# A two-layer diffusion step on one core: up-projection halves of 320 instead of 322 columns, and two instructions queued elsewhere

## The chip, the cores and the metric

The kernel runs on one core of a Trainium2 chip. The metric is the device time of one execution in microseconds; the median of three runs before the change is 1535.12 us (1534.82 to 1535.30).

## The reference

One inference step of a two-layer trunk in float32: 512 latent tokens and 128 prompt (context) tokens of width 1024. Layer 0 mixes tokens by neighbourhood attention (NA) with a learned position bias, layer 1 by grouped-query attention (GQA) with rotary positions. After each mixer stands a gated feed-forward block (FFN) with a width-3 convolution along the tokens. Six modulation rows per layer come from a conditioning vector.

```python
def conv_ffn(h, w_up, conv_w, conv_b, w_down):       # w_up 1024 x 5632, w_down 2816 x 1024
    u = h @ w_up
    up = jnp.pad(u, ((0, 0), (1, 1), (0, 0)))
    u = up[:, :-2] * conv_w[0] + up[:, 1:-1] * conv_w[1] + up[:, 2:] * conv_w[2] + conv_b
    a, gt = jnp.split(u, 2, axis=-1)
    return (jax.nn.silu(a) * gt) @ w_down

for l in range(2):
    shift/scale/gate rows = split(silu(c) @ ada_w[l] + ada_b[l], 6)      # for c and for c_ctx
    h = rmsnorm(x, norm_mix_pre) * (1 + scale) + shift
    o = neighbourhood_attention(...) if l == 0 else gqa(...)
    x = x + gate * rmsnorm(o @ w_o, norm_mix_post)
    h = rmsnorm(x, norm_ffn_pre) * (1 + scale) + shift
    x = x + gate * rmsnorm(conv_ffn(h, ...), norm_ffn_post)
# outputs: both token groups, and the prompt's keys and values of both layers
```

The convolution pads each of the two token groups on its own: there is a zero on both sides of the latents and of the prompt.

## The kernel before

Every float32 product is made of three passes in a reduced format: each operand is split into a high part (a cast on ScalarE: `wh`, `ahi`, `oh`) and a low part (a subtraction on VectorE or GpSimd: `wl`, `alo`, `ol`), and high x high, high x low and low x high add up in one accumulator.

**Order.** The instructions of TensorE run in the order of the text (`pe` chains them). On the other engines a planner, which simulates the program, orders the ready instructions by their place in the text. `behind(a, b)` puts a behind b in its engine's queue without a wait for b's end, and `keep_in_program_order` (`pin=True` in `wsplit`) puts an instruction behind the one that stands before it in the text on its engine. All large weights come by SP's DMA queue into four rotating buffers `wr`.

**NA and its output projection.** While the heads are worked off, a stream of items (`stream`, `na_qk_items`, `na_v_items`) makes queries, keys and values of the next heads in small parts; `fill` takes one part. The last item is the keys of the last head pair. `OW` says behind which of its parts (0 to 7) the output projection's weights 0, 1 and 2 of the first column half are fetched and split (`m0.weights`): behind parts 0, 2 and 4. The last part (i = 7) copies the prompt's keys out of the accumulator (`kp`, ScalarE), for a transpose on TensorE (`tk`, in `tail`) that follows, and then forms the key tiles `kh` and `kl`.

**The up-projection.** It is a Winograd form of Strassen's scheme: the 1024 rows of the contraction and the 640 tokens are cut in halves, and value and gate columns form the third pair, so that 7 block products stand for 8. The tokens are laid out with a zero column behind the latents and behind the prompt, `GAP` = 642, and the halves have `TH` = 322 columns (2 x 322 = 644). `Halves` builds the token blocks B; the first `PLAIN` = 2 rows of chunks of 128 output columns are made without the scheme (`plain0`, `plain1`), the other 20 by the seven products (1, 2, 6, 3, 7, 5, 4 in `evict`), whose order in the loop is 6, 5, 1 of the next row, 7, 2 of the next row, 3, 4. Each product is 12 matmuls of TH columns. The results are added into `C`, [128, 4 x 322 + 3], a new tile of three rotating ones for each row, with a GpSimd memset of its three zero columns. The columns of the gap come out as zeros since the token columns there are zero.

**Around the products.** For each row p, VectorE forms sums of weight blocks in place (`block_sums`, L1313 to L1316), ScalarE casts them (L1291) and GpSimd subtracts (`wl`, `vl`, L1292). The convolution (`conv`) is one ScalarE operation and two on VectorE (L1368, L1371), for the value part with a Silu and for the gate part with the multiplication by it (L1382, `act`), over 2 x 322 columns in the accumulator `t`. The result goes to memory and is read again for the down-projection (`load_dn`, `ain`, `ahi`, `alo`, accumulators `acc`), which begins right behind the last row and takes the accumulator banks that `t` leaves.

**Modulation rows.** `ada_work` runs between the products. The last row, (1, 5), is made during the last rows of FFN 1: an add out of the accumulator (L320), the multiplication by a norm's gain (L323), and two DMAs.

Of the kernel before, what the change touches and what calls it, by code (L numbers as in the profile page):

```python
# [19 lines left out]
P = 128  # L20
# [19 lines left out]
NPT = 6  # L40
NPK = 6
NAR = 2
OW = {0: 0, 2: 1, 4: 2}
OEARLY = 2
TH = 322
PLAIN = 2
NC = 3
QKH = (slice(0, 256), slice(256, T))
# [56 lines left out]
def hybrid_step(ctx: ExitStack, tc: tile.TileContext, A, O):  # L105
# [106 lines left out]
    class Halves:  # L212

        EDGE = (0, 190, TH)

        def __init__(self, keep, tmp):
            self.B = {n: [keep.tile([P, 4, TH], F32R, name=f"B{n}{i}") for i in range(2)] for n in ("11", "21")}
            self.h = tmp.tile([P, KC, 2 * TH], F32, name="hF")  # L220
            for c0, c1 in ((NS, NS + 1), (GAP - 1, 2 * TH)):
                nc.gpsimd.memset(self.h[:, :, c0:c1], 0.0)

        def block(self, i, j, c0=0, c1=TH):
            return self.h[:, 4 * i : 4 * i + 4, TH * j + c0 : TH * j + c1]
# [44 lines left out]

    gain_of = {1: "norm_mix_pre", 2: "norm_mix_post", 4: "norm_ffn_pre", 5: "norm_ffn_post"}

    arows = []

    def ada_work(p, rawp, group, steps, todo, wait=1, sizes=()):

        bias = p.tile([P, 256], F32, name="abias")
        gr = p.tile([P, 256], F32, name="again")  # L280
        nc.gpsimd.memset(bias, 0.0)
        nc.gpsimd.memset(gr, 0.0)

        def quarters(row):
            return row.rearrange("(j c) -> j c", j=4)

        loads = deque((l, idx, k) for l, idx in todo for k in range(KC))
        raws = deque()

        def load():  # L290
            if loads:
                l, idx, k = loads.popleft()
                raw = rawp.tile([P, D], F32, tag="wr", name="wr")
                i = nc.sync.dma_start(raw, A["ada_w"][l, k * P : k * P + P, idx * D : idx * D + D])
                if queue:
                    behind(i, queue.pop())
                raws.append((l, idx, k, raw))

        for _ in range(group):
            load()  # L300
        for _ in range(wait):
            yield
        sizes = iter(sizes)
        while raws:
            n = min(len(raws), next(sizes, len(raws)))
            for _ in range(n):
                l, idx, k, raw = raws.popleft()
                if k == 0:
                    for q in range(2):
                        nc.sync.dma_start(bias[q::32, :], quarters(A["ada_b"][l, idx * D : idx * D + D]))  # L310
                        if idx in gain_of:
                            nc.sync.dma_start(gr[q::32, :], quarters(A[gain_of[idx]][l]))
                    ps = bk.get("ada")
                for j in range(4):
                    mm(ps[32 * j : 32 * j + 32, 0:256], scolp[:, 2 * k : 2 * k + 32], raw[:, 256 * j : 256 * j + 256],
                       start=k == 0, stop=k == KC - 1)
                if k < KC - 1:
                    continue
                orow = p.tile([P, 256], F32, tag="arow", name="arow")
                arows.append(nc.vector.tensor_add(orow, ps[:, 0:256], bias))  # L320
                bk.put(ps)
                if idx in gain_of:
                    nc.vector.scalar_tensor_tensor(  # L323
                        orow, orow, 1.0 if idx in (1, 4) else 0.0, gr, op0=ALU.add, op1=ALU.mult
                    )
                for q in range(2):
                    nc.scalar.dma_start(quarters(modrow[l][idx][q]), orow[q::32, :])
            for i in range(steps):
                for _ in range(n if steps == 1 else i < n):
                    load()  # L330
                yield
# [516 lines left out]
    with l_na:  # L848
# [50 lines left out]
        def na_qk_items(p):  # L899
# [34 lines left out]
            def part(which, half, k0):  # L934
# [12 lines left out]
                if which == 0:  # L947
                    if half == 0:
                        d["qs"] = [ap.tile([P, QW], F32R, tag=f"qs{b}", name=f"qs{b}") for b in range(2)]
                    pieces = [(slice(64 + cs.start, 64 + cs.stop), slice(0, nq))]  # L950
                    if half == 1:
                        pieces.append((slice(0, 64), slice(NS - 64 - cs.start, NS - cs.start)))
                    for qc, pc in pieces:
                        for b in range(2):
                            own, oth = own_oth(b)
                            nc.scalar.activation(d["qs"][b][own, qc], pp[own, pc], AF.Copy, scale=-0.125)
                    for qc, pc in pieces:
                        for b in range(2):
                            own, oth = own_oth(b)
                            q = d["qs"][b]  # L960
                            nc.vector.scalar_tensor_tensor(
                                q[oth, qc], pp[own, pc], -0.125, f32(q[own, qc]),
                                op0=ALU.mult, op1=ALU.subtract,
                            )
                else:
                    if half == 0:
                        d["kh"] = [ap.tile([P, T + P], F32R, tag=f"kh{b}", name=f"kh{b}") for b in range(2)]
                        d["kl"] = kls[p % 2]
                        tk = bk.get("tk")
                        turn(tk[:, 0:P], d["kc"], ident)  # L970
                        k_put(CTX * P, CTX * P + P, tk[:, 0:P])
                        bk.put(tk)
                    if half == 1:
                        d["kp"] = ap.tile([P, P], F32, tag="kc", name="kp", bufs=2)
                        nc.scalar.copy(d["kp"], pp[:, NS - cs.start : T - cs.start])
                    k0 = cs.start + P * (cs.start >= CTX * P)
                    k_put(k0, k0 + nq, pp[:, 0:nq])
                    if half == 1:
                        qk_of[p] = (d["qs"], d["kh"], d["kl"])
# [137 lines left out]
        def stream():  # L1117
            items[0][0]()
            tail = None
            for n, (load, parts) in enumerate(items):  # L1120
                for i, part in enumerate(parts):
                    part()
                    if n + 1 == len(items) and i in OW:
                        m0.weights(0, OW[i], None if i == 4 else nc.gpsimd)
                    if i == 1 and n + 1 < len(items):
                        items[n + 1][0]()
                    if i == 4 and tail:
# [95 lines left out]
    h1p = hp1.enter_context(pool("h1"))  # L1223
    xmpool = xmp.enter_context(pool("xm", 2))
    hT = Halves(h1p, xmp.enter_context(pool("hf")))
    fin = Finish(0, 2, x_in, lambda t: xres[0][t], (0, 4, 3, NS + 1), hT, xmpool, 6)
    for u in range(4):
        m0.weights(1, u, (None, nc.gpsimd)[u % 2])
    for t in range(NT):
# [8 lines left out]
    def ffn(l, hT, hT_close, xold, xnew, nxt, todo, late, late_close, side, back, first, fin0, after=None):  # L1238
# [33 lines left out]
        with ExitStack() as s2:  # L1272
# [48 lines left out]
                done.add((p, i))  # L1321
                fetch()

            banks, cs, ts, small, outs, taken, marks = {}, {}, {}, {}, deque(), [], {}

            def block_product(u, w, h, b, first, last=True, lows=False):

# [21 lines left out]
            def sums(p):  # L1349

                if p not in cs:
                    c = cs[p] = sw.tile([P, 4 * TH + 3], F32, tag="C", name="C", bufs=NC)
                    nc.gpsimd.memset(c[:, 0 :: 2 * TH + 1], 0.0)
                return cs[p]

            def block(p, i, j):
                c0 = 1 + (2 * TH + 1) * i + TH * j
                return sums(p)[:, c0 : c0 + TH]

            def conv(part, p):  # L1360
                c, n = sums(p), p + part * FC
                t = ct.tile([P, 2, 512], F32, tag="t", name="t", bufs=1)[:, :, 0:TH]

                def taps(d):
                    c0 = 1 + (2 * TH + 1) * part + d
                    return c[:, c0 : c0 + 2 * TH].rearrange("p (a b) -> p a b", a=2)

                nc.scalar.activation(t, taps(0), AF.Identity, bias=cw[:, 3, n : n + 1], scale=cw[:, 1, n : n + 1])  # L1368
                for w, d in ((2, 1), (0, -1)):
# [3 lines left out]

            def conv_value(p):
                t = conv(0, p)
                ts[p] = up.tile([P, 2, TH], F32, tag="sl", name="sl")
                nc.scalar.activation(ts[p], t, AF.Silu)

            def conv_gate(p):
                t = conv(1, p)  # L1380
                o = up.tile([P, 2, TH], F32, tag="act", name="act", bufs=3)
                marks[4] = nc.vector.tensor_mul(o, t, ts.pop(p))  # L1382
                outs.append((p, o.rearrange("p a b -> p (a b)")[:, 0:GAP]))
                cs.pop(p)

            def evict(m, p, u):
# [7 lines left out]
                elif m == 5:  # L1394
                    copied("v5", p, u)
                elif m == 7:
                    marks[7] = nc.vector.tensor_add(block(p, 1, 1), u, small.pop(("v5", p)))
                elif m == 3:
                    marks[3] = nc.vector.tensor_add(block(p, 0, 1), u, small.pop(("u2", p)))  # L1399
                    bk.put(banks.pop(("z", p)))  # L1400
                    conv_value(p)
                else:
# [20 lines left out]
            def plain1(p, i):  # L1423
# [1 line left out]
                x = banks.pop(("p", p, i))  # L1425
                block_product(x[:, 0:TH], ws[p, i], 1, "22", False)
                block_product(x[:, 0:TH], ws[p, i], 0, "1", False)
                nc.scalar.copy(block(p, i, 1), x[:, 0:TH])
                bk.put(x)

            fetch()
# [83 lines left out]
                            next(ada, None)  # L1515
            if ada:
                drain(ada)
            store()
            bk.drop(2)
        bk.add(psy.enter_context(pool("psy", space=PSUM)), 4)  # L1520
# [469 lines left out]
    fin = Finish(1, 2, lambda t: xres[1][t], lambda t: xres[2][t], (1, 4, 3, NS + 1), hT, xmpool, 6, "right")  # L1990
    for u in range(4):
        m1.weights(1, u, (None, nc.gpsimd)[u % 2])
    for t in range(NT):
# [81 lines left out]
```

## Time and profile before

| | |
|---|---|
| median of 3 runs | 1535.12 us |
| profiled execution, its own time | 1534.98 us |
| its span | 1533.2 us |
| mean granted TensorE clock | 0.997 |
| busy: PE, PEld, DVE, ACT, POOL | 1511.1, 1344.2, 1017.5, 853.5, 701.2 us |
| FFN 0's products, about | 354 to 655 us of the span |
| FFN 1's products, about | 1090 to 1375 us of the span |

The span runs from the first to the last instruction of one profiled execution. Engines: PE is TensorE's matmuls, PEld its weight loads, DVE VectorE, ACT ScalarE, POOL GpSimd, SP the queue that issues most DMAs. A group's row gives line, engine, operation, output<-inputs, shapes and count, then busy time, the mean time of one in ns, and the idle time before it with what ended it. A timeline row gives start, duration, engine, line and operation. Matmuls overlap: a duration of 312 ns does not mean that the next one starts 312 ns later.

### The profile page before, as it was taken

The numbers are of one execution on the slowest core, as the hardware profiler recorded it, in microseconds if no ns is written. First come the engines' busy times: TensorE is split into PE (matmuls) and PEld (weight loads), VectorE is DVE, ScalarE is ACT, GpSimd is POOL, SyncE is SP. The second block draws the span as 40 slices with busy tenths as digits, with TensorE's granted clock in tenths as the row PEclk, the third lists the DMA queues.
The fourth block names the chain that finished last, engine by engine and source line by source line (L and its number), as shares of the span: only waits on it lengthen the run. The fifth ranks groups of instructions, "written<-read, shape, count | busy, mean of one in ns | idle before, by whom it ended". The sixth has DMA issues, their size and how long they took to land.

```text
span 1533.2 us, 26148 instructions
## 1 busy us (share of the span) xinstructions
PE 1511.1 (99%) x9710; PEld 1344.2 (88%) x9710; DVE 1017.5 (66%) x1653; ACT 853.5 (56%) x1628; POOL 701.2 (46%) x602
## 2 busy tenths in 40 slices
PE   7999999999999999999999999999999999999998
PEld 5999989779999999988887878878999999998886
DVE  5544343659776666765747878763988887885454
ACT  5665564655655555644545447763665665564443
POOL 1745554332355445534544544532335665543433
PEclk9999999999999999999999999999999999999999
DMA  9755444263665664387574420015433335349564
GB/s 350 187 143 144 124 134 110 63 217 100 199 225 188 209 198 150 128 291 266 188 225 149 124 83 29 1 59 188 139 127 111 118 113 157 125 156 311 185 223 131
DMA packets 196666, 243.99 MB, mean 159 GB/s; under 512 B 11484, under 2 KB 153020, under 8 KB 196540
## 3 DMA queue, kind: packets, MB, share of 16 engines
q1 hardware_dynamic: 186924, 235.85, 47.5%
q10 hardware_dynamic: 9616, 6.48, 2.4%
q8 instruction: 76, 1.25, 0.3%
q14 instruction: 50, 0.41, 0.1%
HBM read 214.38 MB, written 26.34 MB: 157 GB/s over the span
## 4 chain that ended last, share of the span: by engine, by line
PE 63%; DVE 8%; issue 2%; ACT 1%; DMA 1%; POOL 1%; ACTq 0%; DVEq 0%; POOLq 0%
PE acc L117 19%; PE ux L117 17%; PE uz L117 8%; PE uy L117 4%; PE gp L117 4%; PE y L117 3%; PE po L117 2%; PE s L117 2%; PE tp L120 2%; PE ada L117 2%; DVE B L249 1%; DMA wr<-in_ffn_w_up 1%; DVE wl L178 1%; DMA gn<-in_gqa_k_norm 1%; DVE nmg L1796 1%
## 5 line engine op out<-in xcount | busy, mean ns | idle before, releaser
L178 POOL TENSOR_TENSOR wl<-wr,wh 128x1024 fp32r<-128x1024 f32 x70 | 170.8, 2444 | 235.0 <-ACT wh L176 224.2
L117 PE MATMUL ux<-B,wh 128*128 128x322 f32 x832 | 200.6, 312 | 0.7 <-ACT u L1347 0.4
L1292 POOL TENSOR_TENSOR wl<-wr,wh 128x1024 fp32r<-128x1024 f32 x76 | 181.5, 2410 | 42.1 <-ACT wh L1291 38.3
L1371 DVE SCALAR_TENSOR_TENSOR t<-C,cw,t 128x644 f32<-128x644 f32 x176 | 156.3, 888 | 50.8 <-ACT t L1368 50.3
L117 PE MATMUL acc<-wh,ahi 128*128 128x512 f32 x440 | 172.2, 391 | 0.6 <-DVE act L1382 0.6
L117 PE MATMUL acc<-wh,alo 128*128 128x512 f32 x440 | 172.3, 392 | 0.0
L117 PE MATMUL acc<-wl,ahi 128*128 128x512 f32 x440 | 172.1, 391 | 0.0
L176 ACT CAST wh<-wr 128x1024 fp32r<-128x1024 f32 x138 | 143.4, 1048 | 35.1 <-DMA wr<-in_ffn_w_down 24.8
L117 PE MATMUL uz<-B,wh 128*128 128x322 f32 x640 | 155.9, 312 | 0.0
L117 PEld LDWEIGHTS ux<-B,wh 128*128 128x128 f32 x832 | 143.7, 189 | 4.2 <-ACT u L1347 1.3
L1260 DVE TENSOR_TENSOR alo<-ain,ahi 128x384 fp32r<-128x384 f32 (+1 forms) x88 | 76.8, 889 | 89.0 <-ACT ahi L1258 88.5
L117 PE MATMUL ux<-B,wl 128*128 128x322 f32 x416 | 129.5, 311 | 0.0
L117 PE MATMUL qk<-hT,wh 128*128 128x384 f32 (+1 forms) x512 | 122.4, 315 | 0.0
L117 PEld LDWEIGHTS uz<-B,wh 128*128 128x128 f32 x640 | 111.0, 189 | 2.9 <-issue 0.8
L1291 ACT CAST wh<-wr 128x1024 fp32r<-128x1024 f32 x84 | 85.0, 1049 | 47.0 <-DVE wr L1316 46.7
L1292 POOL TENSOR_TENSOR vl<-wr,vh 128x1024 fp32r<-128x1024 f32 x38 | 98.5, 2591 | 20.0 <-ACT vh L1291 19.7
L1368 ACT ACTIVATE t<-C,cw 128x644 f32<-128x644 f32 x88 | 78.6, 893 | 44.1 <-DVE C L1399 31.6
L178 DVE TENSOR_TENSOR wl<-wr,wh 128x1024 fp32r<-128x1024 f32 x68 | 88.8, 1319 | 20.5 <-ACT wh L176 19.8
L1258 ACT CAST ahi<-ain 128x384 fp32r<-128x384 f32 (+1 forms) x88 | 39.8, 461 | 110.1 <-PE acc L117 94.1
L117 PE MATMUL uz<-B,wl 128*128 128x322 f32 x320 | 99.6, 311 | 0.4 <-POOL wl L1292 0.3
L117 PEld LDWEIGHTS acc<-wh,ahi 128*128 128x128 f32 x440 | 82.7, 188 | 18.6 <-issue 1.0
L117 PEld LDWEIGHTS acc<-wh,alo 128*128 128x128 f32 x440 | 82.6, 188 | 17.9 <-DVE alo L1260 0.2
(264 smaller groups left out, 3899.0 us busy)
## 6 DMA issues: line engine op xcount, KB each, us to landing
wr<-in_ffn_w_up SPq DMA_DIRECT2D x88, 512.0 KB
wr<-in_ffn_w_down SPq DMA_DIRECT2D x88, 512.0 KB
wr<-in_ada_w SPq DMA_DIRECT2D x72, 512.0 KB
act<-act SPq DMA_DIRECT2D x44, 321.0 KB
wr<-in_na_w_qkv SPq DMA_DIRECT2D x24, 512.0 KB
mod<-modrow SPq DMA_DIRECT2D x20, 512.0 KB
ain<-act SPq DMA_DIRECT2D x44, 192.0 KB
wf<-in_ada_w SPq DMA_DIRECT2D x16, 512.0 KB
```

The source lines that it names most:

```text
L117: pe(nc.tensor.matmul(*a, **k))
L120: pe(nc.tensor.transpose(*a, **k))
L176: i = nc.scalar.copy(hi, raw)
L178: j = (low or nc.vector).tensor_sub(lo, raw, f32(hi))
L249: return nc.vector.tensor_sub(lo, src, f32(hi))
L1258: pin(nc.scalar.copy(hi[:, 0 : c1 - c0], ain[:, 0 : c1 - c0]))
L1260: i = nc.vector.tensor_sub(lo[:, 0 : c1 - c0], ain[:, 0 : c1 - c0], f32(hi[:, 0 : c1 - c0]))
L1291: nc.scalar.copy(hl[0], src)
L1292: return low.tensor_sub(hl[1], src, f32(hl[0]))
L1368: nc.scalar.activation(t, taps(0), AF.Identity, bias=cw[:, 3, n : n + 1], scale=cw[:, 1, n : n + 1])
L1371: nc.vector.scalar_tensor_tensor(t, taps(d), cw[:, w, n : n + 1], t, op0=ALU.mult, op1=ALU.add))
L1796: self.red[i] = nc.vector.tensor_reduce(nm, sv, axis=AX.XY, op=ALU.min)
```

## The change

1. **Halves of 320 columns.** `TH` becomes T // 2 = 320: the token blocks hold the 640 tokens without gap columns. The gaps now stand in `C` alone: three fixed tiles [128, 2 x 643 + 2] are made once a layer, their zero columns set once, and rows take them in turn. A result of the second half is written in two pieces (`pieces`), 192 columns of latents and 128 of the prompt one column further on: two VectorE adds instead of one for products 3 and 7, and two ScalarE copies instead of one in `plain1`. The convolution works on 2 x 321 columns (`CH`). The prompt's tokens start at column 512 instead of 513, and the second half's first pieces are 192 and 128 wide instead of 190 and 132 (`EDGE`).
2. **NA's third output weight.** It is no longer fetched and split behind part 4 of the last item but inside part 7, right behind the copy `kp`. Its cast and its subtraction (on VectorE, as before) are pinned there.
3. **The last modulation row's closing.** In FFN 1 its multiplication by the gain (L323) is put behind the last activation (`marks[4]`) in VectorE's queue.

```diff
-OW = {0: 0, 2: 1, 4: 2}
+OW = {0: 0, 2: 1}
-TH = 322
+TH = T // 2
+CH = GAP // 2
...
-        EDGE = (0, 190, TH)
+        EDGE = (0, NS - TH, TH)
...
-            for c0, c1 in ((NS, NS + 1), (GAP - 1, 2 * TH)):
-                nc.gpsimd.memset(self.h[:, :, c0:c1], 0.0)
...
                 if idx in gain_of:
-                    nc.vector.scalar_tensor_tensor(
+                    gained[:] = [nc.vector.scalar_tensor_tensor(
                         orow, orow, 1.0 if idx in (1, 4) else 0.0, gr, op0=ALU.add, op1=ALU.mult
-                    )
+                    )]
...
                         nc.scalar.copy(d["kp"], pp[:, NS - cs.start : T - cs.start])
+                        if p == KC - 1:
+                            m0.weights(0, 2)
...
-                        m0.weights(0, OW[i], None if i == 4 else nc.gpsimd)
+                        m0.weights(0, OW[i], nc.gpsimd)
...
-    fin = Finish(0, 2, x_in, lambda t: xres[0][t], (0, 4, 3, NS + 1), hT, xmpool, 6)
+    fin = Finish(0, 2, x_in, lambda t: xres[0][t], (0, 4, 3, NS), hT, xmpool, 6)
...
                 if p not in cs:
-                    c = cs[p] = sw.tile([P, 4 * TH + 3], F32, tag="C", name="C", bufs=NC)
-                    nc.gpsimd.memset(c[:, 0 :: 2 * TH + 1], 0.0)
+                    if p < NC:
+                        c = sw.tile([P, 2 * (GAP + 1) + 2], F32, name=f"C{p}")
+                        for o in (0, 1, 2 + NS):
+                            nc.gpsimd.memset(c[:, o :: GAP + 1], 0.0)
+                        held.append(c)
+                    cs[p] = held[p % NC]
                 return cs[p]
 
             def block(p, i, j):
-                c0 = 1 + (2 * TH + 1) * i + TH * j
+                c0 = 2 + (GAP + 1) * i + TH * j
                 return sums(p)[:, c0 : c0 + TH]
+
+            def pieces(p, i):
+                c, c0 = sums(p), 2 + (GAP + 1) * i
+                for a, b, o in ((0, NS - TH, TH), (NS - TH, TH, TH + 1)):
+                    yield slice(a, b), c[:, c0 + o + a : c0 + o + b]
...
                 elif m == 7:
-                    marks[7] = nc.vector.tensor_add(block(p, 1, 1), u, small.pop(("v5", p)))
+                    v = small.pop(("v5", p))
+                    for c, dst in pieces(p, 1):
+                        marks[7] = nc.vector.tensor_add(dst, u[:, c], v[:, c])
                 elif m == 3:
-                    marks[3] = nc.vector.tensor_add(block(p, 0, 1), u, small.pop(("u2", p)))
+                    v = small.pop(("u2", p))
+                    for c, dst in pieces(p, 0):
+                        marks[3] = nc.vector.tensor_add(dst, u[:, c], v[:, c])
                     bk.put(banks.pop(("z", p)))
                     conv_value(p)
...
-                nc.scalar.copy(block(p, i, 1), x[:, 0:TH])
+                for c, dst in pieces(p, i):
+                    nc.scalar.copy(dst, x[:, c])
                 bk.put(x)
...
                 drain(ada)
+                if not nxt:
+                    behind(gained[0], marks[4])
             store()
```

More of the change, by code (lines that the diff above doesn't have):

```diff
@@ L271, in hybrid_step @@
     gain_of = {1: "norm_mix_pre", 2: "norm_mix_post", 4: "norm_ffn_pre", 5: "norm_ffn_post"}
-    arows = []
+    arows, gained = [], []
     def ada_work(p, rawp, group, steps, todo, wait=1, sizes=()):
@@ L1322, in sum_parts @@
                 fetch()
-            banks, cs, ts, small, outs, taken, marks = {}, {}, {}, {}, deque(), [], {}
+            banks, cs, ts, small, outs, taken, marks, held = {}, {}, {}, {}, deque(), [], {}, []
             def block_product(u, w, h, b, first, last=True, lows=False):
@@ L1351, in sums @@
                 if p not in cs:
-                    c = cs[p] = sw.tile([P, 4 * TH + 3], F32, tag="C", name="C", bufs=NC)
-                    nc.gpsimd.memset(c[:, 0 :: 2 * TH + 1], 0.0)
+                    if p < NC:
[4 more added lines that the diff above has]
+                    cs[p] = held[p % NC]
                 return cs[p]
             def block(p, i, j):
-                c0 = 1 + (2 * TH + 1) * i + TH * j
+                c0 = 2 + (GAP + 1) * i + TH * j
                 return sums(p)[:, c0 : c0 + TH]
+            def pieces(p, i):
+                c, c0 = sums(p), 2 + (GAP + 1) * i
+                for a, b, o in ((0, NS - TH, TH), (NS - TH, TH, TH + 1)):
+                    yield slice(a, b), c[:, c0 + o + a : c0 + o + b]
             def conv(part, p):
                 c, n = sums(p), p + part * FC
-                t = ct.tile([P, 2, 512], F32, tag="t", name="t", bufs=1)[:, :, 0:TH]
+                t = ct.tile([P, 2, 512], F32, tag="t", name="t", bufs=1)[:, :, 0:CH]
                 def taps(d):
-                    c0 = 1 + (2 * TH + 1) * part + d
-                    return c[:, c0 : c0 + 2 * TH].rearrange("p (a b) -> p a b", a=2)
+                    c0 = 2 + (GAP + 1) * part + d
+                    return c[:, c0 : c0 + GAP].rearrange("p (a b) -> p a b", a=2)
                 nc.scalar.activation(t, taps(0), AF.Identity, bias=cw[:, 3, n : n + 1], scale=cw[:, 1, n : n + 1])
@@ L1375, in conv_value @@
                 t = conv(0, p)
-                ts[p] = up.tile([P, 2, TH], F32, tag="sl", name="sl")
+                ts[p] = up.tile([P, 2, CH], F32, tag="sl", name="sl")
                 nc.scalar.activation(ts[p], t, AF.Silu)
@@ L1380, in conv_gate @@
                 t = conv(1, p)
-                o = up.tile([P, 2, TH], F32, tag="act", name="act", bufs=3)
+                o = up.tile([P, 2, CH], F32, tag="act", name="act", bufs=3)
                 marks[4] = nc.vector.tensor_mul(o, t, ts.pop(p))
-                outs.append((p, o.rearrange("p a b -> p (a b)")[:, 0:GAP]))
+                outs.append((p, o.rearrange("p a b -> p (a b)")))
                 cs.pop(p)
@@ L1989, in hybrid_step @@
     hT = Halves(h3p, xmp.enter_context(pool("hf", 1, "right")))
-    fin = Finish(1, 2, lambda t: xres[1][t], lambda t: xres[2][t], (1, 4, 3, NS + 1), hT, xmpool, 6, "right")
+    fin = Finish(1, 2, lambda t: xres[1][t], lambda t: xres[2][t], (1, 4, 3, NS), hT, xmpool, 6, "right")
     for u in range(4):
```

## The prediction

> **What bounds the kernel now.** I read the page's first part, then the waits, then the chain of work that ended last, and last the windows of the stretches that the chain names.
>
> ```profile
> span 1533.2 us, 26148 instructions
> ...
> PE 1511.1 (99%) x9710; PEld 1344.2 (88%) x9710; DVE 1017.5 (66%) x1653; ACT 853.5 (56%) x1628; POOL 701.2 (46%) x602
> ```
>
> TensorE is busy for all but 22 us of the span, so time can come only from less TensorE work or from those few gaps. The waits (total, times, longest) name the two gaps that the change's last two parts touch:
>
> ```profile
> PE tk L120 <- ACT kp L975: 1.7, 1, 1.7
> ...
> PE acc L117 <- DVE act L1382: 0.6, 1, 0.6
> ```
>
> A busy TensorE can still be kept waiting in small steps, so I ask the chain (start, length, what) where TensorE itself sets the pace in the two FFNs:
>
> ```profile
> 392.61 2.05 PE ux L117 x12
> ...
> 655.35 88.41 PE acc L117 x390
> ...
> 1128.53 2.06 PE ux L117 x12
> ...
> 1143.10 1.79 PE uy L117 x12
> ...
> 1173.63 2.40 POOL wl L1292
> 1176.07 1.90 PE uz L117 x11
> ...
> 1194.02 1.78 PE uy L117 x12
> ...
> 1256.26 1.78 PE uy L117 x12
> ```
>
> The chain is TensorE from 392.61 to 655.35 and from 1176.07 to 1371.3. Just before 392.61 and 1128.53, from 1144.9 to 1176.07 and from 1371.3 to 1383.7 it runs through VectorE, ScalarE and GpSimd. The windows (length, then busy time of PE, PEld, DVE, ACT, POOL) agree:
>
> ```profile
> 354.10:392.60 38.50, 37.97 (x257) 37.16 (x256) 36.73 (x44) 22.31 (x39) 9.42 (x12) 1.00 0.42 130
> 392.60:655.30 262.70, 262.59 (x1941) 249.44 (x1942) 187.53 (x265) 152.62 (x221) 138.35 (x77) 1.00 0.58 186
> ...
> 1176.10:1371.30 195.20, 195.20 (x1349) 192.08 (x1350) 160.53 (x199) 116.94 (x170) 115.18 (x60) 1.00 0.42 133
> 1371.30:1383.70 12.40, 11.84 (x60) 9.88 (x60) 11.72 (x15) 5.85 (x8) 2.49 (x1) 1.00 0.54 184
> ```
>
> VectorE is full (36.73 of 38.50, 11.72 of 12.40) where the chain leaves TensorE, and TensorE is full elsewhere.
>
> **Two columns fewer in each product.** A layer has 2 plain chunk rows of 2 x 4 products and 20 Winograd rows of 7, 12 matmuls each: 192 + 1,680 = 1,872, so 3,744 in both layers go from 322 to 320 columns. Today's spacing: from 1194.02 to 1256.26 lie five rows of 84, 62.24 / 420 = 148.2 ns. What two columns are worth comes from other widths, by the timeline and by the group at exactly 320:
>
> ```profile
> 46.23 0.28 PE L117 MATMUL qk<-hT,wh 128*128 128x256 f32 x1
> ...
> 48.97 0.45 PE L117 MATMUL qk<-hT,wh 128*128 128x256 f32 x2
> 49.26 0.34 PE L117 MATMUL qk<-hT,wl 128*128 128x384 f32 x1
> ...
> 53.14 0.45 PE L117 MATMUL qk<-hT,wh 128*128 128x384 f32 x2
> ```
> ```profile
> L117 PE MATMUL s<-gkl,gq 128*128 128x320 f32 x128 | 29.2, 309 | 0.0
> ```
>
> Twenty-three matmuls of 256 start between the first two rows (119.1 ns each), 22 of 384 between the last two (176.4 ns): 0.447 ns a column, 0.89 ns for two. The 320-column scores come in pairs, so busy time per pair, 29.2 / 64 = 456 ns, less one duration of 309 leaves a spacing of 147.3 ns, 0.9 below 148.2. I take 0.88 ns. It counts only where the chain is TensorE: all but 3 of the 138 products from 392.61 on (1,620 matmuls), 9 products from 1128.53 to 1144.9 (108), and 107 products less one matmul from 1176.07 to 1371.3 (1,283): 3,011 x 0.88 = **2.65 us gained**. The other 733 run beside a full VectorE and are costed at nothing. In those start-ups some ten whole-block operations of VectorE a layer (`sums`, `parts`) go from 1,288 to 1,280 elements, about 8 ns each by VectorE's rows below (133 ns for 128 elements): **0.15 us** for both layers.
>
> A rule speaks against this term. The Trainium skill, TensorE: Matmul & The Clock Gate, section Back-to-back issue gap, gives the sustained spacing of load-and-matmul pairs as about 81 ns at 128 columns and 131 ns at 512, which is 0.13 ns a column; by it the term would be an estimated 0.8 us. This trace disagrees: 88.41 us for 390 matmuls of 512 columns is 226.7 ns.
>
> **Split evictions.** The adds of products 3 and 7 become two, of 192 and 128 elements.
>
> ```profile
> L1399 DVE TENSOR_TENSOR C<-uz,u 128x322 f32<-128x322 f32 x40 | 19.8, 494 | 32.7 <-PE uz L117 32.7
> ...
> L320 DVE TENSOR_TENSOR arow<-ada,abias 128x256 f32<-128x256 f32 x9 | 3.8, 421 | 10.4 <-PE ada L117 10.4
> ...
> L930 DVE TENSOR_TENSOR kl<-tk,kh 64x128 fp32r<-64x128 f32 x16 | 4.6, 288 | 7.8 <-ACT kh L925 7.7
> ```
>
> 192 lies between 288 and 421 ns, so 355 + 288 = 643 against 494 ns: 0.15 us more in each, 80 times, of which about half is overlap with the next instruction (the 0.48 us add at 1373.69 lets L323 start at 1374.09, below). It is hidden behind waits for TensorE: 32.7 us of idle time stand before product 3's adds alone. The eight copies of the plain rows split likewise on ScalarE (22.31 of 38.50 busy), at nothing. The memset per row leaves GpSimd's queue (nine a layer remain, at the start); nothing is gained, since GpSimd waits for its cast operand anyway. Ends: -0.2 us, and +1.8 us in FFN 1 if the loop below binds.
>
> ```profile
> 1245.74 4.77 POOL L1292 TENSOR_TENSOR wl<-wr,wh 128x1024 fp32r<-128x1024 f32 x2
> 1250.47 2.87 POOL L1292 TENSOR_TENSOR vl<-wr,vh 128x1024 fp32r<-128x1024 f32 x1
> 1257.98 4.77 POOL L1292 TENSOR_TENSOR wl<-wr,wh 128x1024 fp32r<-128x1024 f32 x2
> ```
> ```profile
> 1253.69 0.77 PE L117 MATMUL ux<-B,vl 128*128 128x322 f32 x4
> ```
> ```profile
> 1166.50 0.68 DVE L1313 TENSOR_TENSOR wr<-wr 128x512 f32<-128x512 f32 x1
> 1251.78 2.12 DVE L1313 TENSOR_TENSOR wr<-wr 128x512 f32<-128x512 f32 x1
> ```
>
> VectorE's block sums, ScalarE's casts and GpSimd's subtractions form a loop of 12.24 us a row (1245.74 to 1257.98) against TensorE's 12.45, which becomes 12.38. GpSimd's vl ends at 1253.34, 0.35 us before TensorE wants it. So the cover is there but thin.
>
> **The last modulation row's closing.** In FFN 1 its gain multiply (L323) goes behind the last activation (L1382).
>
> ```profile
> 1372.16 0.55 DVE L1260 TENSOR_TENSOR alo<-ain,ahi 128x384 fp32r<-128x384 f32 x1
> ...
> 1374.09 0.42 DVE L323 SCALAR_TENSOR_TENSOR arow<-arow,again 128x256 f32<-128x256 f32 x1
> 1374.42 2.76 DVE L1260 TENSOR_TENSOR alo<-ain,ahi 128x384 fp32r<-128x384 f32 x1
> ...
> 1382.75 0.83 DVE L1382 TENSOR_TENSOR act<-t,sl 128x644 f32<-128x644 f32 x1
> ```
> ```profile
> 1374.28 2.49 POOL L178 TENSOR_TENSOR wl<-wr,wh 128x1024 fp32r<-128x1024 f32 x1 [6.55 <-ACT wh L176]
> ```
>
> VectorE gets back 0.33 us (1374.09 to 1374.42). More hangs on it: the subtraction that follows took 2.76 instead of 0.55 us, ending when GpSimd's operation did. Without L323, and with two split adds ahead (0.07 each), it starts near 1374.23, 0.05 us before GpSimd. If it wins, the chain to the activation is about 2 us shorter and the whole wait of 0.6 us goes; next late is then nothing, TensorE has its operands. If it loses, it still ends after GpSimd and nothing is won. The ends are 0 and 0.6 and the margin is too thin to call: **0.3 us**. The row's two DMAs go to ScalarE's queue some 9 us later and SP's loads of that modulation with them; their first reader is the finish of the first down-projection group, over 80 us on, so 0.
>
> The Trainium skill, SBUF — State Buffer, section SBUF: two separate sides, says that the VectorE and GpSimd port pair is an exclusive lock, held for the whole instruction by whichever starts first. The 2.76 us agrees with it; by that rule this term is 0.6 and not 0.3 if the 0.05 us are real.
>
> **The third output weight.** Its cast stood ahead of the prompt's key copy on ScalarE:
>
> ```profile
> 277.54 1.04 ACT L176 CAST wh<-wr 128x1024 fp32r<-128x1024 f32 x1
> 278.61 0.27 ACT L975 COPY kp<-qk 128x128 f32<-128x128 f32 x1
> ```
> ```profile
> 289.23 0.30 PE L120 MATMUL tp<-ident,pp 128*128 128x128 f32 x1 [0.45 <-ACT p L1051]
> ```
> ```profile
> 287.95 1.04 POOL L769 TENSOR_TENSOR pp<-pp,rcp 128x512 f32<-128x512 f32 x1 [3.84 <-DVE rcp L768]
> ```
> ```profile
> 273.00:287.00 14.00, 12.28 (x70) 10.83 (x69) 10.98 (x26) 13.81 (x38) 7.81 (x8) 1.00 0.24 80
> ```
>
> The copy moves up by about 1.0 us and the 1.7 us wait shrinks as much. But the same work stays on ScalarE, 13.81 of 14.00 us busy, and its exponentials feed pp, which TensorE already awaits at 289.23. I expect that wait to grow by what the first one loses: **0**, between 1.0 gained and 0.3 lost (VectorE's subtraction follows the later cast). The weight's DMA has only other output weights around it on SP.
>
> **Sum.** 2.65 + 0.15 + 0.3 = 3.1 us off the profiled execution's 1534.98, 1531.9; the median of the runs, 1535.12, stands 0.14 above that execution: **1532.0 us**, all but exactly 0.2%, which is about what a measurement of this kernel can tell from no change.
>
> **Rivals.**
> 1. Two columns bring more. The line from 256 (119.1) to 512 (226.7) gives 146.0 ns at 320 columns; 322 stands 1.4 above its own place on it. If 320 falls on the line, 2.2 x 3,011 = 6.6 us: 1528.4. Against: the 320-column row, 147.3.
> 2. The change does not do what it says: spacing does not follow single columns. Then 0.45 us is left: 1534.7. Against: the 0.9 ns above.
> 3. The row loop takes over in FFN 1. 12.24 plus two split adds of 0.07 is 12.38, TensorE's new pace; FFN 1's 1,283 x 0.88 = 1.1 us would go: 1533.1.
> 4. Slower. The split adds push a block sum into GpSimd's long operation, 2.12 instead of 0.68 us: 1.44 a row against 0.21 of slack, 1.2 lost. From the third such row of FFN 1 on it eats the whole gain, from the sixth it is slower by over 0.2%; in every second row (7), 8.6 - 3.1 = 5.5 us lost: 1540.6. Against: VectorE idles before the adds.
>
> **How the numbers follow.** Chances: forecast 0.53, rivals 0.10, 0.12, 0.16, 0.09. The forecast case alone spans 1530.8 to 1533.0 (the closing's 0 and 0.6, 0.83 to 0.95 ns, NA's ends in part) and more than half of it lies beyond 0.2%, the bound being 1532.05. With rival 1 and a little of rival 3 that makes 0.46 faster; slower 0.09; the rest the same. The range reaches to rivals 2 and 3 and two thirds of the way to rival 1, 1529.6 to 1534.8, and leaves rival 4 and most of rival 1 out.
>
> **What would show it.** Right: rows of 84 matmuls 12.37 to 12.39 us apart; the kp wait near 0.7 and the wait at pp's turn near 1.4; the last alo near 0.55 us. Wrong: TensorE waits for wl, vl or C inside the rows, or rows still 12.45 apart.

## The result, and the profile after

The changed kernel takes 1531.28 us (median of 11 runs, 1529.61 to 1532.2), the kernel before 1534.81 in the same comparison (11 runs, 1533.18 to 1535.3). The ratio is 0.9975, 95% interval 0.9967 to 0.9983: faster by 3.5 us. The forecast was 1532.0 in a range of 1529.6 to 1534.8. The sum came out nearly right, but not by its terms: two were too small, one had the wrong sign, and two losses stood at places that it had at nothing.

The waits of TensorE after (releaser; total, times, longest):

```profile
PE ux L118 <- DVE C L1409: 1.6, 2, 0.9
...
PE tk L121 <- ACT kp L974: 0.8, 1, 0.8
PE ux L118 <- ACT u L1348: 0.8, 2, 0.4
...
PE sp L118 <- DVE kl L929: 0.4, 1, 0.4
...
PE acc L118 <- DVE act L1392: 0.3, 1, 0.3
```

The kp wait halved, as forecast; new are 1.6 us for product 7's adds (L1409) and 0.4 for kl, the low half of NA's last keys (`sp` are the prompt's scores made from it). A list of waits doesn't say what a wait costs in the end. TensorE issues the same matmuls in the same order in both kernels, so the same matmul can be found in both timelines, and the difference of the two starts shows where time was won and lost. Rows of the timeline (start, length), before and then after:

```profile
38.49 0.87 PE L117 MATMUL vp<-wh,hT 128*128 128x256 f32 x5
405.02 1.35 PE L117 MATMUL ux<-B,vh 128*128 128x322 f32 x8
437.14 0.31 PE L117 MATMUL uy<-B,vh 128*128 128x322 f32 x1
640.95 0.31 PE L117 MATMUL uy<-B,vh 128*128 128x322 f32 x1
743.60 1.04 PE L120 MATMUL tr<-ident,xm 128*128 128x128 f32 x8
1124.63 0.31 PE L117 MATMUL uz<-B,wh 128*128 128x322 f32 x1
1181.41 0.31 PE L117 MATMUL uy<-B,vh 128*128 128x322 f32 x1
1371.13 0.31 PE L117 MATMUL uz<-B,wh 128*128 128x322 f32 x1
1526.15 0.40 PE L117 MATMUL acc<-wh,alo 128*128 128x512 f32 x1
```
```profile
38.87 0.87 PE L118 MATMUL vp<-wh,hT 128*128 128x256 f32 x5
405.73 1.33 PE L118 MATMUL ux<-B,vh 128*128 128x320 f32 x8
438.31 0.31 PE L118 MATMUL uy<-B,vh 128*128 128x320 f32 x1
639.98 0.31 PE L118 MATMUL uy<-B,vh 128*128 128x320 f32 x1
743.39 1.04 PE L121 MATMUL tr<-ident,xm 128*128 128x128 f32 x8
1123.96 0.31 PE L118 MATMUL uz<-B,wh 128*128 128x320 f32 x1
1180.66 0.31 PE L118 MATMUL uy<-B,vh 128*128 128x320 f32 x1
1368.63 0.31 PE L118 MATMUL uz<-B,wh 128*128 128x320 f32 x1
1522.65 0.40 PE L118 MATMUL acc<-wh,alo 128*128 128x512 f32 x1
```

Each column of the table is what one stage gained (-) or lost (+) against the kernel before, from such rows: for the changed kernel, for the same kernel profiled a second time (e12, below), and for each part alone.

| kernel | start to 38 | to 405 (NA) | to 437 (FFN 0's first groups) | to 641 (its rows) | to 744 (its end) | to 1124 | to 1181 (FFN 1's first groups) | to 1371 (its rows) | to the last matmul |
|---|---|---|---|---|---|---|---|---|---|
| after | +0.38 | +0.33 | +0.46 | -2.14 | +0.76 | -0.46 | -0.08 | -1.75 | -1.00 |
| after, again (e12) | -0.78 | +0.31 | +0.46 | -2.15 | +0.75 | +0.11 | -0.09 | -1.76 | -1.00 |
| columns alone (e1) | -0.73 | +0.21 | +0.46 | -2.14 | +0.77 | +0.14 | -0.05 | -1.77 | -0.98 |
| weight alone (e2) | -0.73 | +0.17 | -0.01 | 0.00 | 0.00 | +0.07 | +0.01 | 0.00 | -0.02 |
| closing alone (e3) | -0.91 | +0.44 | -0.01 | -0.01 | 0.00 | -0.44 | +0.02 | 0.00 | -0.96 |

Two profiles of one kernel differ by 1.16 us in the first stage and by 0.57 in the one from 744 to 1124; closing alone has 0.43 between 38 and the transposes at 279, where its edit isn't. Those stages scatter with the run. In the second stage the scatter lies between 80 and 95 us alone: 0.41 us of closing alone's 0.44 arose there, and 0.83 in e7 and 1.38 in e6 (below), none of which has an edit there; the other profiles in the table differ by at most 0.02 in that stretch. The other stages, and the second one behind 95 us, repeat to 0.02 us in those two profiles, finer than any comparison of times here, whose intervals are about 0.2% (3 us) wide. The experiments are therefore read by stage, and their times only stand beside it.

### The profile page after: what moved, and what is told of

The parts are those of the page before. It is cut to its first block, busy times and chain, and to the rows that moved or that the text cites. A ratio compares the mean times of both kernels' runs of the same rounds, so it can differ in the third digit from the quotient of the medians.

```text
span 1529.5 us, 26196 instructions
## 1 busy us (share of the span) xinstructions
PE 1506.5 (98%) x9710; PEld 1338.6 (88%) x9710; DVE 1029.7 (67%) x1733; ACT 853.6 (56%) x1636; POOL 701.1 (46%) x572
## 4 chain that ended last, share of the span: by engine, by line
PE 66%; DVE 7%; issue 1%; ACT 1%; POOL 1%; DMA 0%; DVEq 0%; POOLq 0%; ACTq 0%
PE acc L118 19%; PE ux L118 17%; PE uz L118 9%; PE gp L118 5%; PE uy L118 4%; PE y L118 3%; PE po L118 2%; PE s L118 2%; PE tp L121 2%; PE ada L118 2%; DVE B L248 1%; DVE wl L179 1%; DVE nmg L1813 1%; DVE t L1381 0%; DVE pk L1832 0%
## 5 line engine op out<-in xcount | busy, mean ns | idle before, releaser
L118 PE MATMUL ux<-B,wh 128*128 128x320 f32 x832 | 198.7, 311 | 0.9 <-ACT u L1348 0.8
L1381 DVE SCALAR_TENSOR_TENSOR t<-C,cw,t 128x642 f32<-128x642 f32 x176 | 156.0, 886 | 48.6 <-ACT t L1378 48.0
L118 PE MATMUL uz<-B,wh 128*128 128x320 f32 x640 | 154.6, 310 | 0.0
L1261 DVE TENSOR_TENSOR alo<-ain,ahi 128x384 fp32r<-128x384 f32 (+1 forms) x88 | 80.2, 928 | 85.3 <-ACT ahi L1259 84.3
L118 PE MATMUL ux<-B,wl 128*128 128x320 f32 x416 | 128.8, 310 | 0.0
L1378 ACT ACTIVATE t<-C,cw 128x642 f32<-128x642 f32 x88 | 78.5, 892 | 42.1 <-DVE C L1413 33.5
L118 PE MATMUL uz<-B,wl 128*128 128x320 f32 x320 | 99.0, 309 | 0.0
L118 PEld LDWEIGHTS acc<-wl,ahi 128*128 128x128 f32 x440 | 82.6, 188 | 17.9
```

What stands on the lines that cost most here:

```text
L118: pe(nc.tensor.matmul(*a, **k))
L1261: i = nc.vector.tensor_sub(lo[:, 0 : c1 - c0], ain[:, 0 : c1 - c0], f32(hi[:, 0 : c1 - c0]))
L1381: nc.vector.scalar_tensor_tensor(t, taps(d), cw[:, w, n : n + 1], t, op0=ALU.mult, op1=ALU.add))
```

## The experiments

**Each part alone (e1, e2, e3).** e1 is the changed kernel with parts 2 and 3 taken back:

```diff
-OW = {0: 0, 2: 1}
+OW = {0: 0, 2: 1, 4: 2}
...
-                        if p == KC - 1:
-                            m0.weights(0, 2)
...
-                if not nxt:
-                    behind(gained[0], marks[4])
```

e2 and e3 are the kernel before with part 2 and with part 3.

> Part 1 alone: halves of 320 columns with the split evictions, NA's third output weight and the last row's closing as before. If the parts add as the forecast had them (closing worth 0.3, NA weight 0): 0.3 us above the changed kernel, so near 1531.6, with rows of the up-projection 12.33 us apart and the wait of product 4 for product 7's second piece (0.93 and 0.69 us) still there. If the closing is worth the 0.6 us of acc's old wait: 0.6 above. If NA's weight brought time too, 1 us or more above; if it costs time, level with the changed kernel or below it.

> Part 2 alone on the kernel before: NA's third output weight behind the prompt's key copy. The forecast's 0: within 0.3 us of 1534.8, tk's wait down by about 0.9 us and the same time given back at sp (kl), tp or pp. The optimist's value: 1.0 us faster. The reading of the two traces, from which the changed kernel has lost 0.2 us by pp: 0.0 to 0.3 slower.

> Part 3 alone on the kernel before: the last modulation row's closing behind the last activation. If the closing stood on the path at the end of FFN1 (forecast 0.3, at most 0.6): 0.3 to 0.6 us faster, with alo about 0.55 us long instead of 2.76 and no wait of acc for it. If another operation was as late and takes the wait's place: 0.

Measured, against 1534.56 for the kernel before: e1 1531.05, ratio 0.998 (0.9971 to 0.9989); e2 1534.49, ratio 1.0001 (0.9993 to 1.001); e3 1533.47, ratio 0.9989 (0.998 to 0.9998). The columns carry nearly all of the change. The weight is worth nothing: by stage it gains 0.94 us up to the transpose of kp and loses 1.19 by that of pp, the prompt's attention weights. The closing alone gains 0.96 us, more than its wait of 0.6, all of it behind FFN 1's last product. But e1, with the closing as before, has that gain too (-0.98). The lines that decide are VectorE's alo and GpSimd's wl beside it, first of e1, then of e3:

```profile
1371.10 0.55 DVE L1259 TENSOR_TENSOR alo<-ain,ahi 128x384 fp32r<-128x384 f32 x1
1371.16 2.75 POOL L179 TENSOR_TENSOR wl<-wr,wh 128x1024 fp32r<-128x1024 f32 x1 [7.03 <-ACT wh L177]
```
```profile
1373.19 0.55 DVE L1260 TENSOR_TENSOR alo<-ain,ahi 128x384 fp32r<-128x384 f32 x1
1373.38 2.62 POOL L178 TENSOR_TENSOR wl<-wr,wh 128x1024 fp32r<-128x1024 f32 x1 [6.57 <-ACT wh L176]
```

Whichever starts first holds the other up. Before, GpSimd was first by 0.14 us and alo took 2.76 us. In e1 VectorE is first by 0.06 us (and wl takes 2.75 us against 2.41 in the changed kernel), in e3 by 0.19, in the changed kernel by 0.41 (alo at 1371.36, wl at 1371.77). e1 wins this race by a hair; the closing gives the win a margin. So the two parts' gains don't add.

Nor does the win need the 320 columns. e6, e7 and e9 (below) have 322 or 324 columns and the closing as before; VectorE is first by 0.21, 0.20 and 0.08 us, and each gains 0.96 or 0.97 us behind FFN 1's last product, e9 as follows:

```profile
1375.25 0.55 DVE L1260 TENSOR_TENSOR alo<-ain,ahi 128x384 fp32r<-128x384 f32 x1
1375.33 2.75 POOL L178 TENSOR_TENSOR wl<-wr,wh 128x1024 fp32r<-128x1024 f32 x1 [6.56 <-ACT wh L176]
```

What the kernel before, e2 and e3 have alone is a late start of VectorE's add for the last product 7. It begins 0.38 us behind ScalarE's cast, though both wait for the same product; in the other eleven profiles it is 0.02 or 0.03 us behind. Before:

```profile
1371.37 1.05 ACT L176 CAST wh<-wr 128x1024 fp32r<-128x1024 f32 x1 [2.18 <-PE ux L117]
1371.75 0.49 DVE L1397 TENSOR_TENSOR C<-ux,v 128x322 f32<-128x322 f32 x1 [1.20 <-PE ux L117]
```

Without these 0.35 us VectorE would have been first by about 0.2 us already (an estimate: 0.35 less 0.14). Where they come from is not shown. e3 wins because the multiplication that it moves away had stood there for 0.33 us.

**Are the pieces of the split adds the loss? (e4, e9, e10).** In the changed kernel another operation stands between the two pieces of product 7's add, and TensorE, whose product 4 takes the same bank, waits for the second. VectorE and TensorE in FFN 0, after:

```profile
426.43 0.35 DVE L1409 TENSOR_TENSOR C<-ux,v 128x192 f32<-128x192 f32 x1
426.70 0.82 DVE L1392 TENSOR_TENSOR act<-t,sl 128x642 f32<-128x642 f32 x1
427.43 0.28 DVE L1409 TENSOR_TENSOR C<-ux,v 128x128 f32<-128x128 f32 x1
```
```profile
427.77 0.42 PE L118 MATMUL ux<-B,ah 128*128 128x320 f32 x1 [0.93 <-DVE C L1409]
```

e4 puts the operation behind both pieces, here and at the like place of FFN 1:

```diff
                     evict(m, q, product(m, q))
+                    if m == 7 and (l, q) == (0, 4):
+                        behind(marks[4], marks[7])
+                    elif m == 7 and (l, q) == (1, 2):
+                        behind(taken[3], marks[7])
```

> The changed kernel with the two pieces of product 7's add kept together in VectorE's order at the two places where TensorE waited (FFN0 for the fifth group, FFN1 for the third). If the gap between the pieces is what cost time: 0.93 + 0.69 = 1.6 us less waiting, so 1.3 to 1.6 us faster than the changed kernel, near 1529.8, and no wait of ux for product 7's adds over 0.2. Rival: the operation moved behind the pieces (an activation, a tap) is then late itself, and TensorE waits for it at the next bank: no change.

Measured: 1531.39, ratio to before 0.9978 (0.9969 to 0.9987): nothing gained. By stage the first groups stand at +0.46 in FFN 0, as in the changed kernel, and at +0.28 in FFN 1, 0.36 worse. The waits only moved, by some 10 us in FFN 0 and 30 to 40 in FFN 1 (a fourth, 0.28 us for C, is at 1172):

```profile
426.90 0.42 PE L118 MATMUL ux<-B,ah 128*128 128x320 f32 x1 [0.19 <-DVE C L1409]
436.30 0.42 PE L118 MATMUL ux<-B,wh 128*128 128x320 f32 x1 [0.47 <-ACT u L1348]
...
1162.99 0.41 PE L118 MATMUL uz<-B,wl 128*128 128x320 f32 x1 [0.33 <-POOL wl L1293]
```

e9 has the split without the width (pieces of 190 and 132 in the kernel before), e10 the width without the split:

```diff
+                for a, b in ((0, 190), (190, TH)):
+                    yield slice(a, b), d[:, a:b]
```
```diff
-                for a, b, o in ((0, NS - TH, TH), (NS - TH, TH, TH + 1)):
+                for a, b, o in ((0, TH, TH),):
```

> The kernel before, 322 columns, with the adds of products 7 and 3 and the last copies of the four plain blocks cut in two pieces of 190 and 132 columns: the changed kernel's cut without its width. The forecast's price of the cut, 0: 1534.8 or so, no new wait. What the changed kernel's trace says: TensorE waits 0.7 to 0.9 us for a second piece in the first groups of FFN0 and again in those of FFN1, 1.6 us in all: about 1536.3, rows of the later groups unchanged.

> The changed kernel with those adds and copies in one piece of 320 columns, laid without the zero column between image and prompt (so the convolution reads one column wrong there, and the last column of each half as zero: that part of the result is changed). Width without the cut. If the cut costs what TensorE waits for it: 1.6 us faster than the changed kernel, and no wait of ux for product 7's adds; if VectorE is simply late in the first groups whatever the pieces, as the joined kernel suggests: 0.5 us faster or less, and other waits of ux and uy stay.

(In e10 the prompt's columns stand one place off in the convolution's input; that part of the result is changed.) Measured: e9 1534.54 against 1534.8, ratio 0.9999 (0.999 to 1.0008); e10 1529.95, ratio 0.997 (0.9958 to 0.9981), beside 1531.19, ratio 0.9978 (0.9969 to 0.9986), of the changed kernel in the same comparison, intervals that overlap. e9 has one such wait:

```profile
1135.86 0.42 PE L117 MATMUL ux<-B,ah 128*128 128x322 f32 x1 [0.66 <-DVE C L1404]
```

and yet its stage to 1181 stands at +0.04, and the one to 437 at -0.11: the same matmuls are 0.9 us later behind the wait and level again 45 us on. The wait of 0.31 us for wl at 1176 that the kernel before has is gone there. e10 stands at +0.03 to 437, where the changed kernel has +0.46, but at +0.21 to 1181, where that has -0.08. With 320 columns the split thus costs 0.43 us in FFN 0 and brings 0.29 in FFN 1, over both layers 0.46 - 0.08 - 0.03 - 0.21 = 0.14 us; with 322 columns (e9) it costs nothing. So nearly all of the 1.6 us in the list of waits is made up again, counted over both layers. The expectations that took the waits for the price, in e4, e9 and e10, were wrong. e10's other reading, that the other engines are late whatever the pieces, fits: without the split TensorE waits 0.50 us for ScalarE's copy u at 435.8 and twice 0.32 for GpSimd's wl in FFN 1. Which engine sets the pace of these groups was not isolated.

**What is it in 320 columns? (e5, e6, e7).** e5 keeps 320 columns but lays the rows of all token blocks B (the "sums tiles" below) 322 columns apart, in the line shown and likewise in `begin`; e6 is the kernel before with two of the token blocks, those of products 1 and 2, at 336 columns a row; e7 is the kernel before with 324 columns.

```diff
-keep.tile([P, 4, TH], F32R, name=f"B{n}{i}")
+keep.tile([P, 4, TH + 2], F32R, name=f"B{n}{i}")[:, :, 0:TH]
```
```diff
-keep.tile([P, 4, TH], F32R, name=f"B{n}{i}")
+keep.tile([P, 4, 336], F32R, name=f"B{n}{i}")[:, :, 0:TH]
```
```diff
-TH = 322
+TH = 324
...
-        EDGE = (0, 190, TH)
+        EDGE = (0, NS - TH, TH)
```

> The changed kernel with its sums tiles B laid out at 322 columns a row, 320 of them used. It tells width from the rows' layout: if the matmul's 1.45 ns came from 320 columns being streamed, rows of 84 matmuls stay 12.33 us apart (146.7 ns); if from rows that start on whole multiples of 1280 bytes, those of the products that read B go back to about 148.2 ns and the mean over a row to 147.3 or so (12.37 to 12.40).

> The kernel before, 322 columns, with the two kept sums tiles (those of products 1 and 2) at 336 columns a row. If the rows' layout sets the spacing: products 1 and 2 about 147 ns a matmul, the other five 148.2. If the width does: all seven 148.2.

> The kernel before with halves of 324 columns. If every column costs 0.42 ns (the slope between 512 and 320 columns: 226.7 and 146.7) and 322 lies on a line through 148.2 by an offset of its own: 149.0 ns a matmul. If the stream is rounded up to whole groups of 4 columns: 148.4, the same as 322 columns within 0.2. If a column costs 0.73 ns here (1.46 for two): 149.7.

One run each (1535.18, 1535.04 and 1537.15 us; e5's time lies 3.5 us above its span of 1531.7, the others' 1.8); the answer is in the row stages. First e5, then e6, then e7:

```profile
439.43 0.31 PE L118 MATMUL uy<-B,vh 128*128 128x320 f32 x1
642.00 0.31 PE L118 MATMUL uy<-B,vh 128*128 128x320 f32 x1
1182.77 0.31 PE L118 MATMUL uy<-B,vh 128*128 128x320 f32 x1
1370.95 0.31 PE L118 MATMUL uz<-B,wh 128*128 128x320 f32 x1
```
```profile
438.19 0.31 PE L117 MATMUL uy<-B,vh 128*128 128x322 f32 x1
642.20 0.31 PE L117 MATMUL uy<-B,vh 128*128 128x322 f32 x1
1182.08 0.31 PE L117 MATMUL uy<-B,vh 128*128 128x322 f32 x1
1372.18 0.31 PE L117 MATMUL uz<-B,wh 128*128 128x322 f32 x1
```
```profile
438.60 0.32 PE L117 MATMUL uy<-B,vh 128*128 128x324 f32 x1
642.40 0.31 PE L117 MATMUL uy<-B,vh 128*128 128x324 f32 x1
1183.48 0.31 PE L117 MATMUL uy<-B,vh 128*128 128x324 f32 x1
1374.29 0.31 PE L117 MATMUL uz<-B,wh 128*128 128x324 f32 x1
```

From the first to the second row lie 15 groups of 7 products (1,260 matmuls) of FFN 0, from the third to the fourth 1,248 of FFN 1. The differences, against 203.81 and 189.72 us before:

| kernel | FFN 0's rows | a matmul | FFN 1's rows | a matmul |
|---|---|---|---|---|
| after, 320 columns | 201.67 | -1.70 ns | 187.97 | -1.40 ns |
| e5, 320 columns, rows of 322 | 202.57 | -0.98 ns | 188.18 | -1.23 ns |
| e6, 322 columns, two blocks with rows of 336 | 204.01 | +0.16 ns | 190.10 | +0.30 ns |
| e7, 324 columns | 203.80 | -0.01 ns | 190.81 | +0.87 ns |

With rows of 322 the width brings 0.98 and 1.23 ns of the gain, the layout of the token blocks the rest: 0.72 ns in FFN 0, 0.17 in FFN 1. None of my pure cases holds. Rows of a multiple of 64 bytes are not enough, since e6 (1,344 bytes) got slower; multiples of 128 or 256, as 320 columns have (1,280 bytes), were tried with 320 columns alone. Two columns more cost nothing in one layer and 0.87 ns in the other.

The traces also say that the price differs by product. In FFN 1's rows the mean spacing of starts inside products 2, 3, 4, 6 and 7 hardly varies from row to row (standard deviation at most 0.25 ns); it is 147.8, 147.3, 147.3, 147.8 and 150.7 ns before and 146.4, 147.0, 146.7, 147.3 and 147.1 after: the gain is 0.2 ns in product 3 and 3.7 in product 7. In e6 product 2, expected near 147, stands at 149.3, and product 4, whose block kept its rows of 322, at 148.9. So the width and a block's own rows are not the whole, and the division into width and layout holds for these kernels only. What exactly in the layout counts stays open; where the blocks lie was not varied by itself.

**A better version (e8, e11).** In NA ScalarE works almost without a break up to pp (13.81 of the 14.00 us before 287 in the prediction's window). e8 is e4 with the fourth output weight's cast and subtraction moved out of that stretch, behind head 13's steps. e11 is the changed kernel (pieces not joined) with the same move, and with the third weight behind the last key casts:

```diff
-                        if p == KC - 1:
-                            m0.weights(0, 2)
                     k0 = cs.start + P * (cs.start >= CTX * P)
                     k_put(k0, k0 + nq, pp[:, 0:nq])
+                    if half == 1 and p == KC - 1:
+                        m0.weights(0, 2)
...
-                m0.weights(0, 3)
...
+            if h == 13:
+                m0.weights(0, 3)
```

> The joined kernel with NA's fourth output weight taken from the block behind head 12 to behind head 13's steps, so that its cast (1.06 us of ScalarE) and its low half (1.65 us of VectorE) leave the stretch 275 to 290 us, in which TensorE is busy for 13.23 of 15 us. If ScalarE's unbroken work up to pp sets that stretch: 0.5 to 1.2 us faster than the joined kernel, near 1529.0. Rival: kl and tp, which wait for VectorE and the transposes, keep the time, or the weight is late where it is next: 0, or some tenths slower.

> The changed kernel (pieces not joined) with NA's fourth output weight behind head 13's steps, and its third behind the last key casts instead of ahead of them. If the low half of the third weight (1.65 us of VectorE) is what made sp wait for kl: that wait of 0.4 us goes too, and the stretch from 275 to 292 us gains 1.0 to 1.2 us on the changed kernel, in all about 1530.1. Rival: pp or the transposes take over, and it stands where the joined kernel with the fourth weight moved stood, 0.7 better in that stretch.

> The changed kernel once more, beside the three others on one chip: 1531.3, within 0.7.

Measured: e8 1530.85 against 1535.0, ratio 0.9974 (0.9964 to 0.9985); e11 1530.84 against 1534.8, ratio 0.997 (0.9959 to 0.9982); e12, the changed kernel beside e11, 1531.19. By stage e11 gains 0.94 us on e12 between 38 and 300 us (-0.81 against +0.13), just under the 1.0 to 1.2 expected, and keeps it; all of it arises behind 279 us. Its span is only 0.4 us shorter because its first 38 us came out 0.85 us later, in the stage that scatters; the times alone don't separate the two. e8 gained 0.63 on e4 there (-0.50 against +0.13); the rest, some 0.3, is what the third weight's place adds. (The fourth weight's subtraction takes 1.21 us in e4; the 1.65 us in e8's expectation are the third's.) The window from 275 to 292 us of e11 and then of e12 (length; busy time of PE, PEld, DVE, ACT, POOL):

```profile
275.00:292.00 17.00, 15.88 (x88) 12.26 (x89) 13.02 (x35) 14.15 (x43) 9.04 (x10) 1.00 0.18 66
```
```profile
275.00:292.00 17.00, 15.26 (x84) 11.55 (x84) 14.13 (x35) 14.28 (x40) 9.12 (x10) 1.00 0.34 110
```

TensorE is busy 0.62 us longer in the same 17 us; VectorE has 1.1 us less to do.

## Why the prediction came out right, and where its steps were wrong

**Two columns fewer: right mechanism, size too small.** Forecast 0.88 ns times 3,011 matmuls, 2.65 us; the row stages gave 2.14 + 1.75 = 3.89 us over 2,508 of them, 1.55 ns each, where the forecast had 2.21 us. The rows of 84 matmuls came 12.33 us apart in FFN 1, not 12.37 to 12.39. I had taken the price from other widths and from a group of 320 columns elsewhere, at 147.3 ns. e5 shows that width alone is worth 0.98 and 1.23 ns with rows of 322; the rest comes with the layout, for which the forecast had no term. That 322 columns cost more than their width, rival 1 had in it ("322 stands 1.4 above its own place"). The measured price lay about halfway between the forecast and that rival.

**The start-ups: wrong sign.** Forecast 0.15 us gained there, and 0.44 more for the 503 matmuls of the 3,011 that lie in the first groups and in FFN 0's last products. The first groups lost 0.46 in FFN 0 and gained 0.08 in FFN 1, and the products ahead of 405 lost another 0.18 (in e1 and e12 alike). I had counted the chain's TensorE stretch from 392.61 on as paced by TensorE. From 405 to 427 the faster matmuls did gain 0.25 us; then TensorE met the other engines and lost it again, with the split (0.93 us of wait for C at 427.8) or without (0.50 for u at 435.8, e10). A chain that runs through TensorE there showed only that the others were not yet late.

The loss ahead of 405 looks like one more race between VectorE and GpSimd. Before, GpSimd's small operation `v` (L373) starts 0.18 us ahead of VectorE's wl at 362.18 and takes 0.26 us; in all eight profiles with 320 columns it stands behind wl's start and takes 1.41 to 1.85 us, VectorE's `xm` waits for what follows it, and TensorE loses 0.45 to 0.51 us between 367 and 371. e6, with 322 columns, has 1.40 us there as well and loses 0.31; the five other profiles with 322 or 324 columns have 0.26 or 0.27 us and lose at most 0.02. No run moved that operation alone.

**Split evictions: the price was right, not the reason.** Nothing forecast, 0.14 measured (e10), though 1.6 us of waits appeared and 0.43 lost in one layer stand against 0.29 won in the other: that is luck. The idle 32.7 us before product 3's adds stood in the later groups; in the first ones VectorE waited for product 3 once, for 0.4 us, and the operation between the two pieces was not foreseen.

**The closing: 0.3 forecast, between 0 and 0.6; 0.96 measured (e3).** The upper end was too low, as two rows of the timeline before show:

```profile
1382.75 0.39 PE L117 MATMUL acc<-wh,alo 128*128 128x512 f32 x1
1383.72 0.47 PE L117 MATMUL acc<-wh,ahi 128*128 128x512 f32 x1 [0.59 <-DVE act L1382]
```

The wait is listed with 0.59 us, but the two matmuls start 0.97 us apart instead of 0.23, and the same matmuls of e3 gain a further 0.10 us ahead of this place and 0.10 behind it. The term was not the closing's own either: e1, e6, e7 and e9 win the race without it, and the 0.05 us of lead that the forecast reckoned with were counted from a start 0.35 us late. The forecast had the collision right, but not what decides it.

**What I had at nothing: FFN 0's end.** There the same collision was won before and is lost after. VectorE's alo and GpSimd's wl before, and then after, with TensorE's wait that follows:

```profile
654.36 0.55 DVE L1260 TENSOR_TENSOR alo<-ain,ahi 128x384 fp32r<-128x384 f32 x1
654.79 2.40 POOL L178 TENSOR_TENSOR wl<-wr,wh 128x1024 fp32r<-128x1024 f32 x1 [5.16 <-ACT wh L176]
```
```profile
653.67 2.41 POOL L179 TENSOR_TENSOR wl<-wr,wh 128x1024 fp32r<-128x1024 f32 x1 [4.45 <-ACT wh L177]
654.07 2.43 DVE L1261 TENSOR_TENSOR alo<-ain,ahi 128x384 fp32r<-128x384 f32 x1
663.02 0.47 PE L118 MATMUL acc<-wh,ahi 128*128 128x512 f32 x1 [0.26 <-DVE act L1392]
```

wl waits for ScalarE's cast, which follows TensorE's products; it came 1.12 us sooner. alo stands in VectorE's full queue and came only 0.29 us sooner. VectorE's lead of 0.43 us became a lag of 0.40, alo took 2.43 us, and the stage lost 0.76, of which the list shows 0.26. In all eight profiles of kernels of 320 columns GpSimd is first here (by 0.10 us in e5, whose rows are slower, and 0.27 in e10 without the split), in the kernel before and the five others of 322 or 324 columns it is VectorE. This is rival 4's collision, at a place I hadn't looked at and once instead of in every second row; not the split adds bring it about, as in rival 4, but TensorE's pace, since e10 loses here too (0.74 us) and e9 does not. The Trainium skill, SBUF — State Buffer, section SBUF: two separate sides, has the port pair of VectorE and GpSimd as an exclusive lock for a whole instruction. The rows of both FFNs' ends agree, with 0.55 us for alo where it comes first and 2.40 to 2.76 where it comes second. That the collision and not something else about 320 columns costs the 0.76 us is argued from these rows: here the two always go together, unlike at FFN 1's end. That moving an operation at FFN 0's end, as part 3 does at FFN 1's, would win the 0.76 us back was not tried.

**The weight: 0 forecast; 0.17 lost up to 405 (e2).** The kp wait shrank as forecast, but the time was not given back where I said, by a longer wait for pp (0.47 after, 0.45 before). Nor did that wait reach the 1.4 us that the prediction gave as a sign. The time went at sp, which waits 0.39 us for kl, and at the matmuls and transposes behind it: the weight's low half stands ahead of kl on VectorE (from 280.01 for 1.65 us, after). e11, which moved that, has no wait for kl.

Rival 3, a loop of the other engines that takes over in FFN 1's rows, did not come: with rows at 320 columns they gained the full 1.75 us.

The terms as forecast and as measured, in us gained: rows 2.21 and 3.89; closing 0.3 and 1.00; start-ups with the 503 matmuls 0.59 and -0.56 (0.18, 0.46, less 0.08); FFN 0's end 0 and -0.76; the weight 0 and -0.15; sums 3.1 and 3.42. Errors of both signs cancelled: that the sum fits is luck, that the columns carry it is not.

## What to carry to other kernels

Read a small change by the same instruction's start in both timelines: it resolved 0.05 us where the times needed 1.5. A wait in the list is not its price: behind it other waits may vanish, or the engine may restart late. When the engine in front gets faster, look at each place where two others race for something shared, and count by how little the race is decided now. A race lost by 0.14 us was won under edits that did not aim at it (e6, e7, e9); its gain can't be credited to any one of them.

## What the runs showed of the hardware

With these matmuls a column has no fixed price: 322 to 320 columns saved 1.70 and 1.40 ns in the two layers, 322 to 324 cost -0.01 and 0.87 ns, and laying 320 columns in rows of 322 took 0.72 and 0.17 ns of the gain back. In one and the same kernel, at 322 columns, the spacing differed by product, 147.3 to 150.7 ns in FFN 1's rows. A start 0.06 us ahead of GpSimd's subtraction was enough for VectorE's to take 0.55 us instead of 2.76.
